# Split rings of four pieces and two more load buffers in both expert stages; two of four output blocks stored plainly

## The chip, the cores and the metric

The kernel runs on one core of one Trainium2 chip. The metric is the device time of one execution in microseconds (us); the median of several executions is compared. A profile of one execution is read beside it: PE is TensorE's matmul queue, PEld its weight loads, DVE VectorE, ACT ScalarE, POOL GpSimd and SP SyncE. In the profile, "SPq" is an instruction by which SP issues a transfer, and L107 is line 107 of the kernel.

## The reference

512 tokens of width 1024 pass through two transformer blocks, all in float32. The first has a mixer of forgetting attention and a gated linear recurrence, and then 16 experts of inner width 512, two for each token. The second has a mixer of neighbourhood attention and grouped-query attention, and then 32 experts of inner width 1024, four for each token. Cut to the two expert parts and the end:

```python
# first block: 16 experts, two of one group of four for each token
for e in range(N_EXPERTS):
    h = jax.nn.silu(t @ w_e_gate[e]) * (t @ w_e_up[e])
    y = y + comb[:, e:e + 1] * (h @ w_e_down[e])
...
# second block: 32 experts, four for each token
def expert_block(args):
    xe, e = args
    gu = xe @ w_gu[e] + b_gu[e]
    x_glu = jnp.minimum(gu[:, :D_FF], SWIGLU_LIMIT)
    x_lin = jnp.clip(gu[:, D_FF:], -SWIGLU_LIMIT, SWIGLU_LIMIT)
    act = (x_lin + 1) * (x_glu * jax.nn.sigmoid(SWIGLU_ALPHA * x_glu))
    return act @ w_dn[e] + b_dn[e]
...
x = x + gt1 * rmsnorm(y, g_post_mix[i])          # after the second mixer
...
x = x + gt2 * rmsnorm(f[:B * S].reshape(B, S, D), g_post_ffn[i])   # the end
```

## The kernel before

**Stages.** By the trace, the first block's mixer runs to about 372 us, its experts from 386 to 724, the second block's mixer to about 1260, its experts from 1269 to 2367, and the end to 2399. The weights of the experts (96 MB in the first stage, 384 in the second) are each read once.

**Loads.** One *step* of an experts' stage is one load of 1 MB by `raw` (L102 to L107) from SP's queue into a buffer `wraw`, and the matmuls with it. `experts` (L1274) writes down the order of all steps in the list `seq`: for each expert the parts "gu" (gate and up) and "dn" (down). `moe_pools` (L960) gives the stage `nraw` buffers, seven in the first stage and nine in the second; RAW is the order in which their places are used. The first loads are issued by SP (AHEAD of them) and by POOL (the rest, in the step that BEHIND names; negative steps lie ahead of the first). From there on load n is issued when step n − `nraw` has given its buffer free (`free`, `load`).

**Splits.** Float32 products are made from split numbers. `split` (L115 to L121) turns half a load, a *half piece* of 128 x 1024, into a high part `whi` (ACT, L120) and the rest `wlo` (DVE, L121). Both have rings of `nsplit` places. A half piece takes three matmuls for each product (`mm3`): high by high, low by high, high by low. The splits are written into the program `ahead` = `nsplit` − 1 half steps ahead of the matmuls that use them (`spl`, `held`; SPL for the first ones). A buffer of a split step is free when both its halves are split. Experts with few tokens (`col`, and `rows` in the second stage: 64 or 32 places) use the load as it is, without a split, and free it when PE has used it.

**Around the matmuls.** `x_gather` (L995) has POOL gather an expert's tokens into `xg`; PE turns them (`x_turn`, L1007), ACT and DVE split them (`x_split`, L1014 to L1018). `act`, `act_turn` and `act_split` (L1136 to L1176) make the activation; `y_scatter` (L1199 to L1212) weighs the result into `eo` on ACT and DVE and POOL adds it into the array `Y` in HBM. `hooks` says in which half step each of these is written into the program; all engines work in program order, each on its own queue. Two experts of each stage (PAIRS) run a second block of 64 places with the same weights.

**The ranking of experts** (L853 and on) runs on POOL, DVE, PE and ACT at the start of each stage, since it decides which expert's weights are loaded where.

**The end.** `tail_norm` (in the second mixer, store at L2147) stores x, 512 tokens in four blocks of 128, into the output. `moe2` (L2190 to L2266) calls `experts` and then reads the sums of the experts (`Y2`) back in four blocks, two from SP and two from ACT (L2250); ACT squares them (L2252); DVE multiplies by the gain (L2256 or L2265) and makes the reciprocal root of two blocks at a time (`rsqrt`, L151 to L161); POOL stores all four blocks with a transfer that adds to the output (L2266). `after` loads the gain row (`RW`, L2238) behind the last weights.

Of the kernel before, what the change touches and what calls it, by code (L numbers as in the profile page):

```python
# [11 lines left out]
F32 = mybir.dt.float32  # L12
F32R = mybir.dt.float32r
# [3 lines left out]
AF = mybir.ActivationFunctionType  # L17
OP = mybir.AluOpType
# [7 lines left out]

FIXED = {2: 2, 1: 2}
PAIRS = {2: (7, 16), 1: (4, 7)}
RAW = {2: (7, 8, 1, 3, 0, 4, 5, 6, 2), 1: (0, 1, 2, 3, 4, 5, 6)}
AHEAD = {2: 6, 1: 4}  # L30
BEHIND = {2: (-11, -11, -11), 1: (-6, -6, -6, -6)}
SPL = {2: (-11, -10.5, -10, -9.5, -9), 1: (-0.5, -0.5, -0.5, -0.5, -0.5)}

PLAN = {2: (0, 1, 2, 3, 4, 5), 1: (-4, -3, -1, 0, 1, 2)}

# [6 lines left out]
class Kern:  # L42
# [129 lines left out]
    def consts(self):  # L172
        nc, cp, t = self.nc, self.cp, self.t
        self.ident = cp.tile([128, 128], F32, name="ident")
        make_identity(nc, self.ident)
        self.identb = cp.tile([128, 128], BF, name="identb")
        nc.vector.tensor_copy(self.identb, self.ident)
        self.onesb = cp.tile([128, 128], BF, name="onesb")
        nc.vector.memset(self.onesb, 1.0)
        self.ones = cp.tile([128, 1], F32, name="ones")  # L180
        nc.vector.memset(self.ones, 1.0)
        jp = cp.tile([128, 128], I32, name="jp")
        nc.gpsimd.iota(jp, pattern=[[1, 128]], base=0, channel_multiplier=-1)
        self.tri = cp.tile([128, 128], BF, name="tri")
        nc.vector.tensor_scalar(self.tri, jp, 0.0, None, op0=OP.is_gt)
        self.mtri = cp.tile([128, 128], BF, name="mtri")
        nc.vector.tensor_scalar(self.mtri, jp, 0.0, -NEG, op0=OP.is_gt, op1=OP.mult)
        self.slots = cp.tile([128, 128], F32, name="slots")
        nc.gpsimd.iota(self.slots, pattern=[[1, 128]], base=0, channel_multiplier=0,
                       allow_small_or_imprecise_dtypes=True)  # L190
        self.pcol = cp.tile([128, 1], F32, name="pcol")
        nc.gpsimd.iota(self.pcol, pattern=[[1, 1]], base=0, channel_multiplier=1,
                       allow_small_or_imprecise_dtypes=True)
        self.trash = cp.tile([128, 1], F32, name="trash")
        nc.vector.tensor_scalar(self.trash, self.pcol, 512.0, None, op0=OP.add)
        rank = cp.tile([32, 48], F32, name="rank")
        nc.gpsimd.dma_start(rank, self.dap(t["rank_c"], 0, [[0, 32], [1, 48]]))
        self.rank = {32: rank[:, 0:32], 16: rank[:, 32:48]}
        self.ntrash = cp.tile([128, 1], F32, name="ntrash")
        nc.vector.tensor_scalar(self.ntrash, self.trash, -1.0, None, op0=OP.mult)  # L200
        self.half = cp.tile([128, 2], F32, name="half")
        nc.vector.memset(self.half, 0.0)
        nc.vector.memset(self.half[64:128, 0:1], 1.0)
        nc.vector.memset(self.half[0:64, 1:2], 1.0)
        self.zero1 = cp.tile([128, 1], F32, name="zero1")
        nc.vector.memset(self.zero1, 0.0)
        self.one1 = cp.tile([128, 1], F32, name="one1")
        nc.vector.memset(self.one1, 1.0)
        self.mod1 = self.dp.tile([6, 1024], F32, name="mod1")
        self.mod2 = self.dp.tile([6, 1024], F32, name="mod2")  # L210
        self.modc = self.dp.tile([2, 1024], F32, name="modc")
        self.X1 = self.dp.tile([512, 1024], F32, name="X1")
        self.U1 = self.dp.tile([512, 1024], F32, name="U1")
        self.U2 = self.dp.tile([512, 1024], F32, name="U2")
        self.Y1 = self.dp.tile([640, 1024], F32, name="Y1")
        self.Y2 = self.dp.tile([640, 1024], F32, name="Y2")
        self.VA = self.dp.tile([512, 512], F32, name="VA")
        self.c1 = self.load_silu([t["c"]])
        self.c2 = self.load_silu([t["c_2"], t["c_ctx_2"]])

# [737 lines left out]


    def moe_pools(self, nh):  # L960
        self.nraw, self.nsplit, self.neo = (7, 9)[nh - 1], 6, nh

        order = RAW[nh]
        low = self.slot_pools(range(self.nraw - 2))
        if nh == 2:
            self.esm = self.pool("e_small", 1)
        self.rings(2048, 0, self.nsplit)
        if nh == 1:
            self.esm = self.pool("e_small", 1)
        self.ex = self.pool("e_x", 2)  # L970
        self.ea = self.pool("e_a", 2)
        high = self.slot_pools(range(self.nraw - 2, self.nraw))
        slots = (low + high)
        it = itertools.cycle([slots[i] for i in order])
        self.rw = type("R", (), {})()
        self.rw.tile = lambda shape, dt, name: next(it).tile(shape, dt, name=name)
# [606 lines left out]
    def mixer2(self):  # L1583
# [555 lines left out]
        def tail_norm(c):  # L2139
# [4 lines left out]
            nc.vector.scalar_tensor_tensor(yc, yc, r, xr[c // 2][:, c % 2, :], op0=OP.mult, op1=OP.add)  # L2144
            nc.gpsimd.tensor_mul(xr[c // 2][:, c % 2, :], yc, rows[1])

            nc.gpsimd.dma_start(self.out[0, cs, :], yc)  # L2147
            q = w4t("q4", 1024)
            nc.scalar.activation(q, yc, AF.Square, accum_out=ss[:, 2 * c + 1:2 * c + 2])
            nc.vector.tensor_copy(rr[:, c:c + 1], self.rsqrt(ss[:, 2 * c + 1:2 * c + 2], 1, 1e-6, 1.0 / 1024))  # L2150
# [40 lines left out]
    def moe2(self):  # L2191
# [39 lines left out]
                self.mm(ps, l.bitcast(F32) if col else l, r.bitcast(F32) if col else r, start, False)  # L2231
            return f
        self.U, self.Y = self.U2, self.Y2
        rows = []

        def after():
            rows.append(self.ea.tile([128, 1024], F32, name="eo", bufs=self.neo))
            nc.sync.dma_start(rows[0], self.dap(self.RW, 2048, [[0, 128], [1, 1024]]))  # L2238

        self.experts(32, src_of, 2, bias_of, (), after)  # L2240

# [1 line left out]
        ss = self.lsm.tile([128, 4], F32, name="ssf")  # L2243
        vs = [self.rw.tile([128, self.wn], F32, name="wraw") for _ in range(4)]
        ys, qs = [v[:, 0:1024] for v in vs], [v[:, 1024:2048] for v in vs]
        d = self.rw.tile([128, self.wn], F32, name="wraw")
        d = [d[:, 0:1024], d[:, 1024:2048], ys[2], ys[3]]
        with self.tc.manual_schedule():
            for c in range(4):
                (nc.scalar if c % 2 else nc.sync).dma_start(ys[c], self.Y2[c * 128:c * 128 + 128, :])  # L2250
            for c in range(4):
                nc.scalar.activation(qs[c], ys[c], AF.Square, accum_out=ss[:, c:c + 1])  # L2252
            for c0 in (0, 2):
                if c0 == 0:
                    for c in (0, 1):
                        nc.vector.tensor_mul(d[c], ys[c], row)  # L2256
                r = self.rsqrt(ss[:, c0:c0 + 2], 2, 1e-6, 1.0 / 1024)
                for c in (c0, c0 + 1):
                    k = r[:, c - c0:c - c0 + 1]
                    if c == 0:  # L2260
                        nc.vector.tensor_scalar(d[c], d[c], k, None, op0=OP.mult)
                    elif c == 1:
                        nc.scalar.activation(d[c], d[c], AF.Copy, scale=k)
                    else:
                        nc.vector.scalar_tensor_tensor(d[c], ys[c], k, row, op0=OP.mult, op1=OP.mult)  # L2265
                    nc.gpsimd.dma_start(self.out[0, c * 128:c * 128 + 128, :], d[c], accum_op=OP.add)  # L2266


_INS = ['x', 'c', 'w_ada', 'b_ada', 'w_in', 'b_f', 'conv_w', 'conv_b', 'w_rg', 'b_rg', 'w_ig', 'b_ig',
# [50 lines left out]
```

## Time and profile before

| | us |
|---|---|
| median of three runs | 2403.52 |
| lowest and highest | 2400.86, 2406.54 |
| the profiled run | 2400.73 |
| its span | 2398.9 |

The profile is one execution. Its times are microseconds from the start of the span; 1.8 us of the run lie around the span. A group of rows says which view it comes from. "idle before <-releaser" in brackets is how long the engine had nothing to do before an instruction, and which instruction or transfer ended that. In the views of DMA, GB/s is what all transfers of the core moved.

### The profile page before, as it was taken

The page shows a single profiled execution, that of the slowest core. Times are in us where ns is not written, and L with a number is a line of the kernel's source. Part 1 is how long each engine was busy: PE and PEld are TensorE (multiplying, and loading weights), DVE is VectorE, ACT ScalarE, POOL GpSimd, SP SyncE. Part 2 cuts the span into 40 slices and gives each one's busy share as a digit, 9 for nine tenths or more (in the row PEclk, how much of TensorE's full clock was granted, in tenths as well). Part 3 has the DMA queues.
Part 4 walks back from the last instruction along what each step waited for, and adds up shares of the span by engine and source line. Part 5 has one row for each costly group of instructions (what it writes and reads, how often), then busy time and mean ns, then how long its engine had stood idle before and what let it go on. Part 6 is the DMA issues. An engine that isn't in the chain of part 4 may idle for free. (4 is left out here: it accounts for less than half of the span.)

```text
span 2398.9 us, 31482 instructions
## 1 busy us (share of the span) xinstructions
PE 2123.2 (89%) x11221; PEld 1360.6 (57%) x11221; DVE 1369.1 (57%) x2676; ACT 1012.0 (42%) x1559; POOL 492.8 (21%) x426
## 2 busy tenths in 40 slices
PE   6999986778897999999978999979999799989983
PEld 2655655445566887778866655635556445536520
DVE  5555697444787856654378655535555365527412
ACT  3332444344673544553236444424444244416301
POOL 2001233311212120000025213311232222114201
PEclk9999997889998999999988999989999999999996
DMA  9767547988986423313448999899999899999997
GB/s 292 234 211 249 182 154 267 348 316 283 321 334 209 98 80 114 103 58 127 145 149 317 346 397 386 355 354 396 398 387 397 308 394 394 395 392 397 389 412 241
DMA packets 208291, 679.29 MB, mean 283 GB/s; under 512 B 21260, under 2 KB 61028, under 8 KB 161024
## 3 DMA queue, kind: packets, MB, share of 16 engines
q1 hardware_dynamic: 185280, 607.88, 67.5%
q0 software_dynamic: 22560, 68.28, 10.5%
q8 instruction: 91, 1.49, 0.3%
q10 hardware_dynamic: 288, 1.05, 0.1%
q14 instruction: 72, 0.59, 0.1%
HBM read 641.51 MB, written 35.72 MB: 282 GB/s over the span
## 5 line engine op out<-in xcount | busy, mean ns | idle before, releaser
L121 DVE TENSOR_TENSOR wlo<-wraw,whi 128x1024 fp32r<-128x1024 f32 (+1 forms) x535 | 642.9, 1234 | 380.0 <-ACT whi L120 372.6
L120 ACT ACTIVATE whi<-wraw 128x1024 fp32r<-128x1024 f32 (+1 forms) x535 | 541.9, 1051 | 375.0 <-DMA wraw<-in_w_gu 129.4
L83 PE MATMUL pm<-whi,xh 128*128 128x512 f32 (+1 forms) x704 | 289.5, 412 | 21.2 <-ACT whi L120 21.2
L83 PE MATMUL pm<-wlo,xh 128*128 128x512 f32 (+1 forms) x704 | 284.5, 407 | 13.7 <-DVE wlo L121 13.5
L83 PE MATMUL pm<-wraw,xh 128*32 128x512 f32 (+1 forms) x1344 | 251.9, 633 | 14.6 <-DMA wraw<-in_w_gu 14.6
L1212 POOL DMA_INDIRECT Y<-eo,isc x52 | 119.2, 2292 | 643.0 <-ACT eo L1211 248.6
L83 PE MATMUL pm<-whi,xl 128*96 128x512 f32 (+1 forms) x608 | 245.7, 404 | 0.0
L83 PEld LDWEIGHTS pm<-whi,xh 128*128 128x128 f32 (+1 forms) x704 | 128.9, 183 | 70.0 <-ACT whi L120 28.9
L995 POOL DMA_INDIRECT xg<-U,ig x52 | 92.4, 1776 | 364.7 <-PE pt L1117 133.0
L83 PEld LDWEIGHTS pm<-wlo,xh 128*128 128x128 f32 (+1 forms) x704 | 122.6, 174 | 60.3 <-DVE wlo L121 23.2
L83 PEld LDWEIGHTS pm<-wraw,xh 128*32 128x32 f32 (+1 forms) x1344 | 65.4, 128 | 140.9 <-issue 106.4
L83 PE MATMUL po<-wraw,ah 128*32 128x512 f32 (+1 forms) x672 | 127.6, 624 | 15.1 <-DMA wraw<-in_w_dn 15.1
L83 PEld LDWEIGHTS pm<-whi,xl 128*96 128x96 f32 (+1 forms) x608 | 109.3, 180 | 34.6 <-issue 0.2
L83 PE MATMUL po<-whi,ah 128*96 128x512 f32 (+1 forms) x304 | 122.2, 402 | 2.6 <-ACT ah L1172 2.5
L83 PE MATMUL po<-whi,al 128*96 128x512 f32 (+1 forms) x304 | 120.1, 395 | 1.8 <-DVE al L1174 1.0
L83 PE MATMUL po<-wlo,ah 128*96 128x512 f32 (+1 forms) x304 | 119.6, 393 | 0.0
L1007 PE MATMUL pt<-ident,xg 64*128 64x64 f32 (+3 forms) x416 | 70.7, 296 | 44.2 <-DMA xg<-U,ig 41.3
L1007 PEld LDWEIGHTS pt<-ident,xg 64*128 64x128 f32 (+3 forms) x416 | 56.9, 199 | 90.6 <-issue 41.1
L1018 DVE TENSOR_TENSOR xl<-pt,xh 128x384 fp32r<-128x384 f32 (+1 forms) x48 | 29.5, 615 | 111.1 <-ACT xh L1016 110.8
L1016 ACT ACTIVATE xh<-pt 128x384 fp32r<-128x384 f32 (+2 forms) x56 | 28.6, 511 | 145.9 <-PE pt L1007 137.1
L83 PEld LDWEIGHTS po<-wraw,ah 128*32 128x32 f32 (+1 forms) x672 | 35.6, 126 | 92.3 <-issue 62.2
L83 PE MATMUL px<-hh,whi 128*128 128x512 f32 x192 | 77.3, 403 | 0.6 <-DVE gsum L765 0.6
(624 smaller groups left out, 3872.4 us busy)
## 6 DMA issues: line engine op xcount, KB each, us to landing
wraw<-in_w_gu SPq DMA_DIRECT2D x254, 1024.0 KB
wraw<-in_w_dn SPq DMA_DIRECT2D x127, 1024.0 KB
wraw<-in_w_e_down SPq DMA_DIRECT2D x32, 1024.0 KB
wraw<-in_w_e_up SPq DMA_DIRECT2D x31, 1024.0 KB
wraw<-in_w_e_gate SPq DMA_DIRECT2D x30, 1024.0 KB
wraw<-in_w_in SPq DMA_DIRECT2D x58, 512.0 KB
mz<-in_w_ada SPq DMA_DIRECT2D x80, 256.0 KB
wraw<-in_w_mod SPq DMA_DIRECT2D x26, 512.0 KB
```

The lines of the kernel that those rows point to most:

```text
L83: self.nc.tensor.matmul(out, lhsT, rhs, start=start, stop=stop)
L120: nc.scalar.activation(h, v, AF.Copy)
L121: nc.vector.tensor_sub(l, v, h.bitcast(F32))
L995: self.nc.gpsimd.indirect_dma_start(out=B.xg[0:B.n, :], out_offset=None, in_=self.U, in_offset=bass.IndirectOffsetOnAxis(ap=B.ig[:, :1], a ...
L1007: self.nc.tensor.transpose(B.xt[:, k * n:k * n + n], B.xg[0:n, 4 * h2 + k:1024:8], self.ident[0:n, 0:n])
L1016: nc.scalar.activation(B.xh[:, d, 0:n], pv, AF.Copy)
L1018: nc.vector.tensor_sub(lo, pv, B.xh[:, d, 0:n].bitcast(F32))
L1212: nc.gpsimd.indirect_dma_start(out=self.Y[:, :], out_offset=bass.IndirectOffsetOnAxis(ap=B.isc[:, :1], axis=0), in_=o, in_offset=None, com ...
```

## The change

- `nraw` is 9 and 11 in place of 7 and 9, `nsplit` is 4 in place of 6. In each partition a buffer takes 8 KB and so does one place of both rings together, so the space is the same. RAW names the new order of the buffers.
- POOL issues five loads at the start of each stage in place of three (BEHIND); three half pieces are split ahead of the first matmul in place of five (SPL).
- A new array X3 in HBM takes blocks 0 and 2 of x from `tail_norm`; blocks 1 and 3 go to the output as before. `after` loads X3 by SP behind the gain row.
- At the end DVE multiplies all four blocks by the gain first, then makes one reciprocal root of four columns. Blocks 0 and 2: DVE multiplies by the root, adds x and SP stores plainly. Blocks 1 and 3: ACT multiplies by the root and POOL stores with the adding transfer.

```diff
--- before.py
+++ after.py
@@ -26,10 +26,10 @@
 
 FIXED = {2: 2, 1: 2}
 PAIRS = {2: (7, 16), 1: (4, 7)}
-RAW = {2: (7, 8, 1, 3, 0, 4, 5, 6, 2), 1: (0, 1, 2, 3, 4, 5, 6)}
+RAW = {2: (9, 10, 1, 3, 0, 4, 5, 6, 2, 7, 8), 1: (0, 1, 2, 3, 4, 5, 6, 7, 8)}
 AHEAD = {2: 6, 1: 4}
-BEHIND = {2: (-11, -11, -11), 1: (-6, -6, -6, -6)}
-SPL = {2: (-11, -10.5, -10, -9.5, -9), 1: (-0.5, -0.5, -0.5, -0.5, -0.5)}
+BEHIND = {2: (-11, -11, -11, -11, -11), 1: (-6, -6, -6, -6, -6)}
+SPL = {2: (-11, -10.5, -10), 1: (-0.5, -0.5, -0.5)}
 
 PLAN = {2: (0, 1, 2, 3, 4, 5), 1: (-4, -3, -1, 0, 1, 2)}
 
@@ -215,6 +215,7 @@
         self.Y1 = self.dp.tile([640, 1024], F32, name="Y1")
         self.Y2 = self.dp.tile([640, 1024], F32, name="Y2")
         self.VA = self.dp.tile([512, 512], F32, name="VA")
+        self.X3 = self.dp.tile([256, 1024], F32, name="X3")
         self.c1 = self.load_silu([t["c"]])
         self.c2 = self.load_silu([t["c_2"], t["c_ctx_2"]])
 
@@ -958,7 +959,7 @@
 
 
     def moe_pools(self, nh):
-        self.nraw, self.nsplit, self.neo = (7, 9)[nh - 1], 6, nh
+        self.nraw, self.nsplit, self.neo = (9, 11)[nh - 1], 4, nh
 
         order = RAW[nh]
         low = self.slot_pools(range(self.nraw - 2))
@@ -2144,7 +2145,7 @@
             nc.vector.scalar_tensor_tensor(yc, yc, r, xr[c // 2][:, c % 2, :], op0=OP.mult, op1=OP.add)
             nc.gpsimd.tensor_mul(xr[c // 2][:, c % 2, :], yc, rows[1])
 
-            nc.gpsimd.dma_start(self.out[0, cs, :], yc)
+            nc.gpsimd.dma_start(self.out[0, cs, :] if c % 2 else self.X3[c * 64:c * 64 + 128, :], yc)
             q = w4t("q4", 1024)
             nc.scalar.activation(q, yc, AF.Square, accum_out=ss[:, 2 * c + 1:2 * c + 2])
             nc.vector.tensor_copy(rr[:, c:c + 1], self.rsqrt(ss[:, 2 * c + 1:2 * c + 2], 1, 1e-6, 1.0 / 1024))
@@ -2231,11 +2232,15 @@
                 self.mm(ps, l.bitcast(F32) if col else l, r.bitcast(F32) if col else r, start, False)
             return f
         self.U, self.Y = self.U2, self.Y2
-        rows = []
+        rows, xs = [], []
 
         def after():
             rows.append(self.ea.tile([128, 1024], F32, name="eo", bufs=self.neo))
             nc.sync.dma_start(rows[0], self.dap(self.RW, 2048, [[0, 128], [1, 1024]]))
+            xs.append(self.ex.tile([128, 1024], F32, name="xg"))
+            xs.append(self.ex.tile([128, 8, 128], F32R, name="xh", bufs=3).bitcast(F32).rearrange("p k q -> p (k q)"))
+            for i in range(2):
+                nc.sync.dma_start(xs[i], self.X3[i * 128:i * 128 + 128, :])
 
         self.experts(32, src_of, 2, bias_of, (), after)
 
@@ -2243,27 +2248,25 @@
         ss = self.lsm.tile([128, 4], F32, name="ssf")
         vs = [self.rw.tile([128, self.wn], F32, name="wraw") for _ in range(4)]
         ys, qs = [v[:, 0:1024] for v in vs], [v[:, 1024:2048] for v in vs]
-        d = self.rw.tile([128, self.wn], F32, name="wraw")
-        d = [d[:, 0:1024], d[:, 1024:2048], ys[2], ys[3]]
+        d = [self.rw.tile([128, self.wn], F32, name="wraw") for _ in range(2)]
+        d = [v[:, 1024 * a:1024 * a + 1024] for v in d for a in range(2)]
         with self.tc.manual_schedule():
             for c in range(4):
                 (nc.scalar if c % 2 else nc.sync).dma_start(ys[c], self.Y2[c * 128:c * 128 + 128, :])
             for c in range(4):
                 nc.scalar.activation(qs[c], ys[c], AF.Square, accum_out=ss[:, c:c + 1])
-            for c0 in (0, 2):
-                if c0 == 0:
-                    for c in (0, 1):
-                        nc.vector.tensor_mul(d[c], ys[c], row)
-                r = self.rsqrt(ss[:, c0:c0 + 2], 2, 1e-6, 1.0 / 1024)
-                for c in (c0, c0 + 1):
-                    k = r[:, c - c0:c - c0 + 1]
-                    if c == 0:
-                        nc.vector.tensor_scalar(d[c], d[c], k, None, op0=OP.mult)
-                    elif c == 1:
-                        nc.scalar.activation(d[c], d[c], AF.Copy, scale=k)
-                    else:
-                        nc.vector.scalar_tensor_tensor(d[c], ys[c], k, row, op0=OP.mult, op1=OP.mult)
-                    nc.gpsimd.dma_start(self.out[0, c * 128:c * 128 + 128, :], d[c], accum_op=OP.add)
+            for c in range(4):
+                nc.vector.tensor_mul(d[c], ys[c], row)
+            r = self.rsqrt(ss, 4, 1e-6, 1.0 / 1024)
+            for c in range(4):
+                k = r[:, c:c + 1]
+                o = self.out[0, c * 128:c * 128 + 128, :]
+                if c % 2:
+                    nc.scalar.activation(d[c], d[c], AF.Copy, scale=k)
+                    nc.gpsimd.dma_start(o, d[c], accum_op=OP.add)
+                else:
+                    nc.vector.scalar_tensor_tensor(ys[c], d[c], k, xs[c // 2], op0=OP.mult, op1=OP.add)
+                    nc.sync.dma_start(o, ys[c])
 
 
 _INS = ['x', 'c', 'w_ada', 'b_ada', 'w_in', 'b_f', 'conv_w', 'conv_b', 'w_rg', 'b_rg', 'w_ig', 'b_ig',
```

## Rows read from the trace of the kernel before

**Rows 1.** The page: busy share of the DMA engines, 40 slices of 60 us

```profile
DMA  9767547988986423313448999899999899999997
```

**Rows 2.** Busy PE, PEld, DVE, ACT, POOL, then PEclk, DMA share, GB/s by window

```profile
1380.00:2360.00 980.00, 886.88 (x4287) 484.54 (x4289) 487.14 (x693) 381.68 (x488) 223.32 (x147) 0.96 1.00 385
386.00:724.00 338.00, 289.80 (x1404) 190.64 (x1402) 209.64 (x348) 181.31 (x258) 77.81 (x62) 0.91 0.89 321
```

**Rows 3.** The same view: inside the two pair experts of the second stage

```profile
1551.00:1561.00 10.00, 10.00 (x58) 6.21 (x56) 4.89 (x2) 1.69 (x2) 6.63 (x5) 1.00 0.10 35
1869.00:1879.00 10.00, 10.00 (x58) 6.10 (x57) 4.84 (x2) 0.86 (x1) 5.82 (x5) 1.00 0.11 28
```

**Rows 4.** Timeline of SP's queue at the first pair; GB/s, 40 slices of 1540:1580

```profile
1545.62 0.33 SPq L107 DMA_DIRECT2D wraw<-in_w_gu  x1
1560.62 0.33 SPq L107 DMA_DIRECT2D wraw<-in_w_gu  x1
GB/s 340 422 418 434 418 434 418 434 434 418 352 188 127 21 0 0 0 0 0 0 16 98 270 418 336 254 385 369 418 418 410 426 442 426 418 418 451 336 164 303
```

**Rows 5.** Windows view again: the start of the second experts' stage

```profile
1280.00:1360.00 80.00, 77.37 (x406) 58.91 (x405) 59.48 (x70) 50.33 (x62) 32.52 (x22) 1.00 0.92 327
```

**Rows 6.** Timeline of POOL ahead of both stages: start, us, engine, line, operation

```profile
377.63 0.58 POOL L107 DMA_DIRECT2D wraw<-in_w_e_gate  x1
1269.39 1.07 POOL L995 DMA_INDIRECT xg<-U,ig  x1 [3.34 <-PE pt L1007]
```

**Rows 7.** Timeline of PE, four waits of the first stage; brackets: idle before, releaser

```profile
469.03 0.68 PE L1158 MATMUL pt<-ident,eb 32*128 32x32 f32 x4 [6.29 <-ACT pt L1544]
494.07 0.74 PE L1158 MATMUL pt<-ident,ea 64*128 64x64 f32 x4 [6.04 <-ACT xh L1014]
570.44 0.74 PE L1158 MATMUL pt<-ident,ea 64*128 64x64 f32 x4 [6.11 <-DVE al L1176]
618.05 0.41 PE L83 MATMUL pt<-paux,oh 128*96 128x6 bf16 x4 [3.55 <-ACT xh L1014]
```

**Rows 8.** Timeline of ACT ahead of the end of the second of these waits

```profile
491.13 1.99 ACT L120 ACTIVATE whi<-wraw 128x1024 fp32r<-128x1024 f32 x2
493.14 0.60 ACT L1172 ACTIVATE ah<-pt 128x512 fp32r<-128x512 f32 x1
493.64 0.38 ACT L1014 ACTIVATE xh<-pt 128x256 f32<-128x256 f32 x1
```

**Rows 9.** Groups of splits, 640 to 712 us, and PE's timeline, one matmul triple

```profile
L121 DVE TENSOR_TENSOR wlo<-wraw,whi 128x1024 fp32r<-128x1024 f32 x44 | 52.0, 1219 | 9.1 <-ACT whi L120 9.0
L120 ACT ACTIVATE whi<-wraw 128x1024 fp32r<-128x1024 f32 x44 | 44.8, 1056 | 14.6 <-DMA wraw<-in_w_e_gate 7.2 <-DMA wraw<-in_w_e_up 3.7 <-PE po L83 1.1
611.81 0.39 PE L83 MATMUL pm<-wlo,xh 128*96 128x512 f32 x1
612.50 0.39 PE L83 MATMUL pm<-wlo,xh 128*96 128x512 f32 x1
```

**Rows 10.** DMA issues: gathers of both stages, count, KB or us to landing

```profile
xg<-U,ig POOLq DMA_INDIRECT x16, 6.7
xg<-U,ig POOLq DMA_INDIRECT x29, 9.8
```

**Rows 11.** Timeline of the end; GB/s, 40 slices of 2374:2382 and of 2385:2398

```profile
2377.66 2.36 DVE L2256 TENSOR_TENSOR wraw<-wraw,eo 128x1024 f32<-128x1024 f32 x2 [7.98 <-DMA wraw<-Y]
2381.82 1.06 ACT L2252 ACTIVATE wraw<-wraw 128x1024 f32<-128x1024 f32 x1 [1.89 <-DMA wraw<-Y]
2384.04 0.18 DVE L151 TENSOR_SCALAR rs<-ssf 128x2 f32<-128x2 f32 x1 [1.08 <-ACT wraw L2252]
2386.30 2.48 DVE L2265 SCALAR_TENSOR_TENSOR wraw<-wraw,rs,eo 128x1024 f32<-128x1024 f32 x2
GB/s 0 0 0 0 0 41 225 184 61 328 492 410 348 328 430 369 451 451 369 389 492 369 369 471 451 348 328 492 328 328 532 410 328 328 41 41 20 20 0 0
GB/s 0 151 126 126 202 214 227 214 202 227 176 202 202 189 214 227 202 189 214 202 202 176 202 202 176 214 202 176 189 189 214 227 139 38 0 0 0 0 0 0
```

**Rows 12.** Timeline of SP's queue behind the first pair

```profile
1587.89 11.15 SPq L107 DMA_DIRECT2D wraw<-in_w_gu  x1
```

## The prediction

> **What bounds the kernel now.** I read the page's line of DMA shares first: it is at its top in slices 9 to 12 and nearly all the way from slice 22 on [rows 1]; these are the two experts' stages. The windows view says what this means in each. In the second stage (1269 to 2367 us) the 16 DMA engines are busy 1.00 of the time at 385 GB/s, while PE has 887 of 980 us of work [rows 2]. So DMA sets the pace there, and only a time at which DMA has nothing to do can be won back. In the first stage (386 to 724 us) DMA stands at 0.89 and PE at 290 of 338 us [rows 2]: neither is full, and each short stall has to be looked at by itself.
>
> Where is DMA idle in the second stage? The windows view with 10 us windows shows two holes, one in each expert that runs a second block (the pairs): PE works 10.00 of 10 us and DMA 0.10 and 0.11 [rows 3]. SP's timeline gives the reason: one load is issued at 1545.62, the next at 1560.62 [rows 4]. A load waits for the buffer that the load nine places earlier used; up to 1560 all nine buffers are loaded or in use, the queue runs dry near 1551, and PE is busy with the pair. A third, smaller loss lies at the start: DMA is at 0.92 in the 80 us from 1280 [rows 5].
>
> **The change, part by part.**
>
> *Two more buffers, second stage, pairs.* Load n now waits for step n−11, not n−9. The pair's splits still free buffers while PE works, but the buffers ahead of it run out two loads later. Around the first pair the GB/s line of the DMA view shows 418 to 434 GB/s while loads flow [rows 4], so a load of 1.05 MB takes 2.5 us, and two fill 5.0 us of the 10 us hole. The stage is bound by DMA on both sides of the hole, so every load behind it, and the end, comes 5.0 us earlier. Two pairs: **−10.0**. Lower bound of the gain: splits run two half pieces (one load) later with the short ring, and where the buffers come from splits the net is one load in place of two, so −2.5 each, −5.0 in all. Upper bound: 2.7 us a load at the stage's mean of 385 GB/s [rows 2], −10.9.
>
> *The same at the start of the second stage.* 0.08 of 80 us is 6.4 us of idle DMA [rows 5]. Two loads more ahead are worth 5.0, but they can't win more than the idle there is, and PE works 77.4 of these 80 us, so part of it could come back as PE's own time. I take **−5.0**, ends 0 and −6.4. The first matmuls wait for a gather, and POOL issues the two added loads ahead of it, at 0.58 us each by the first stage's row; POOL's idle of 3.34 us before that gather covers 1.2 us of it [rows 6]. If the cover were gone it would cost +1.2.
>
> *The first stage, its start.* POOL issues five loads in place of three before it starts the ranking that the plan of the experts needs; one issue takes 0.58 us and the ranking follows at once [rows 6]. PE's first expert waits for that chain: **+1.2**.
>
> *The first stage, shorter ring.* The split of a piece (ACT for the high part, DVE for the rest) is written in program order 5 half pieces ahead of its use; now it is 3. ACT and DVE work in order, so what stands behind a burst of splits waits for it. PE has four waits of 3.55 to 6.29 us that end on such an operation: three on ACT, one on DVE [rows 7]. It is the turned input or activation of a small expert, in the first one a norm for the next mixer. In the second wait two high parts, 1.99 us together, run on ACT right ahead of the operations PE needs [rows 8]; the other three have the same picture. With lead 3 two of the splits move behind them: about 2.0 us if ACT is late, 2.4 if DVE is (two of 1219 ns [rows 9]), and I take 2.2 for each of four: **−8.8**. Ends: nothing, if another wait ends at the same time, and −9.6.
>
> *The first stage, fuller queues.* With two loads more in flight, DMA's 0.89 rises a little, and gathers share it: from issue to landing a gather takes 6.7 us here and 9.8 us in the second stage with DMA at 1.00 [rows 10]. A shift of the share by 0.02 of the 0.11 between them is 0.6 us a transfer, and PE's or ACT's long waits end on three gathers or scatters here: **+1.7**. Ends: 0, and +9.3 (3.1 each). This stage too has holes in DMA (0.11 of 338 us [rows 2]), but PE doesn't wait for loads behind them: filling them is worth nothing in my sum, with −5.0 (a pair's gain in the other stage) as the other end.
>
> *Does the ring of four starve PE?* At the tightest place (640 to 712 us) a high part takes 1056 ns and a low part 1219 [rows 9]: 2.3 us from buffer to ready. PE needs 0.69 us for three matmuls [rows 9], and a half piece has six, 1.38 us. Three pieces ahead are 4.1 us, more than 2.3. So no stall in a steady run, with 1.8 us to spare, where five pieces gave 4.6. I set it at nothing, with an upper end of +4 for this stage; in the second one DMA is the bound.
>
> *The end.* Before, all four results are accumulated into the output from POOL's queue. In the DMA view that runs at about 200 GB/s, while the plain loads of the Y rows come at about 400 [rows 11]: 2.6 us and 1.3 us for 0.52 MB. The accumulates begin in the second slice of 0.325 us behind 2385 and end in the 34th, at 2396.05 [rows 11]. Now, step by step: the first two products are made in 2.36 us from 2377.66; the third and fourth wait for rows that arrive at 2381.82, and end at 2384.2. One reciprocal root over four columns takes as long as the one that starts at 2384.04 and ends at 2386.30, 2.3 us, to 2386.5. The first multiply-and-add is 1.24 us (half of 2.48) [rows 11], so the first store is issued at 2387.7 and flows about 2 us later, as before: 2389.7. Two plain and two accumulated blocks take 2 × 1.3 + 2 × 2.6 = 7.8 us, to 2397.5 against 2396.05: +1.4 if they add up. If plain packets run in the gaps of the accumulating ones, four times 1.3 would do, 2394.9, or −1.2. The Y rows, issued from two queues, moved about 400 GB/s, no more than SP's queue alone at the pair [rows 4, 11]; a plain and an accumulating transfer side by side are in no row. The Trainium skill ("DMA: Bandwidth & Descriptors", section "Issuing engines are not separate DMA queues") says that transfers started on several engines run on the same 16 DMA engines and only save issue time; by that rule the end would cost the whole +1.4. I take **+0.8**, nearer to adding up, ends −1.5 and +1.5. The two loads of X3 (1 MB, 2.5 us) stand behind the last weights and land before the Y rows are issued: nothing. The stores to X3 replace stores of the same size: nothing.
>
> **Sum:** −10.0 −5.0 +1.2 −8.8 +1.7 +0.8 = −20.1 us. The profiled run took 2400.73 us, its span 2398.9 and 1.8 around it; the median of the three is 2403.52, 2.8 above the profiled one. A difference holds for either, so I subtract from the median: 2383.4.
>
> **The rivals.**
>
> *Second stage only.* The first stage's waits come from another cause that comes as late (a scatter, the other engine), so the −8.8 are not there; the rest is −11.3: 2392.2. For it: ACT and DVE both have splits in front, so one may come as late as the other. Against: where the row shows it, the splits are the very last thing in front [rows 8], and both engines lose two of them.
>
> *Loads can't be put in flight.* Two more buffers help only if SP can issue into them. Behind the first pair one issue took 11.15 us where its neighbours take 0.33 [rows 4, 12]: with many loads outstanding, SP blocks. If the queue held no more than it does now, a free buffer would be worth nothing at the pairs' rims; but when the hole begins the queue is empty, so only that part of the gain goes that is not yet issued when DMA runs dry. With one load of two, the three places give −2.5 each and the rest stands: −12.6, 2390.9. The Trainium skill ("Perfetto Trace Analysis", section "DMA Instruction — HWDGE (DVE, Sync)") says that an engine starts early when more descriptors are made than its buffer holds; it gives no depth, and the long issue fits a full buffer.
>
> *Slower: the short ring starves PE.* Wherever ACT or DVE is held up in the first stage (by a gather, a scatter, the step from a small expert to a split one), five pieces of cover were 6.9 us, three are 4.1: a hold longer than that reaches PE 2.8 us earlier. Without the −8.8 the rest of the sum is −11.3, so 4 such holds use it up (4 × 2.8 = 11.2). With one in every second of the 16 experts it is 8 × 2.8 − 11.3 = +11.1: 2414.6. For it: DVE is the longest helper and works in order. Against: 1.8 us to spare in the tightest run, and DMA, not PE, is the bound in most of the second stage.
>
> **How the numbers follow.** Forecast (both stages gain) 0.5: 2383.4, with its own range of 2374 to 2391. Second stage only 0.2: 2392. Loads not in flight 0.14: 2391. Starved ring 0.09: 2414.6; the rest (parts cancel) 0.07: 2401. To leave out no more than 2 in 10 I take 2373 to 2400. Less than 0.2% (4.8 us) is about what can't be told from no change here. Faster than 2398.7: 0.81; within: 0.1; slower than 2408.3: 0.09.
>
> **What would show it.** In the pairs DMA must be idle for 5 us where it was 10, and the gap on SP must shrink to about 10 us. In the first stage PE's four waits must be 2 us shorter. At the end two stores must be seen on SP's queue and the last bytes at 2397.5 less the gain ahead. Wrong would be: PE waiting for a high or low part where it did not, or an SP queue that is blocked when DMA runs dry.

## The result and the profile after

| | before | after |
|---|---|---|
| median, us | 2402.19 | 2377.99 |
| lowest and highest of four | 2399.26, 2406.54 | 2377.08, 2381.31 |
| profiled run: span | 2398.9 | 2379.5 |

The kernel before has a fourth run here, so its median is 1.3 us below the one that the forecast started from. The ratio of the times is 0.990 (95% interval 0.9881 to 0.9919): 24 us less, where 20 were forecast. The profiled run of the changed kernel is the longest of its four; its span is only 19.4 us shorter. Read by stages, from the timeline of PE (the start of its first matmul with a weight of a stage to the start of its last), that is put right:

| us | before | after | difference |
|---|---|---|---|
| up to the first gather of the first experts' stage | 374.2 | 379.6 | +5.4 |
| from there to PE's first such matmul | 11.75 | 11.91 | +0.2 |
| first experts' stage | 336.9 | 323.2 | −13.7 |
| second mixer, to PE's first matmul of the next stage | 546.6 | 547.1 | +0.5 |
| second experts' stage | 1096.5 | 1082.4 | −14.1 |
| to the loads of Y | 8.3 | 8.3 | 0.0 |
| from the loads of Y to the end of the span | 24.7 | 26.9 | +2.3 |

The first line has nothing to do with the change: that part holds the same work, and over the profiles of all the kernels below it took 374.2 to 379.6 us. So the two experts' stages carry the gain, 14 us each.

The page of the changed kernel, its line of DMA shares in 40 slices:

```profile
DMA  8767446988976423323448999999999999999996
```

From slice 23 on DMA is full as before [rows 1], and the slices of the two pairs (26 and 32), which were at 8, are at 9. The windows view of the changed kernel (the columns of rows 2): the first stage, the start of the second, and 16 us about the hole of each pair:

```profile
391.00:715.00 324.00, 288.55 (x1406) 190.21 (x1405) 210.69 (x348) 183.27 (x258) 74.38 (x62) 0.93 0.92 335
1272.00:1352.00 80.00, 76.61 (x388) 58.07 (x387) 60.65 (x71) 50.31 (x60) 27.97 (x20) 1.00 0.97 350
1539.00:1555.00 16.00, 15.29 (x88) 8.63 (x87) 6.66 (x5) 4.51 (x8) 7.77 (x7) 1.00 0.57 210
1849.00:1865.00 16.00, 15.32 (x87) 9.10 (x89) 6.16 (x5) 4.51 (x8) 7.75 (x7) 1.00 0.79 297
```

And the two holes in the kernel before, with windows placed by the same step of the stage (rows 3 have only their cores):

```profile
1549.00:1565.00 16.00, 16.00 (x93) 9.46 (x92) 7.05 (x6) 5.45 (x8) 8.29 (x7) 1.00 0.40 140
1866.00:1882.00 16.00, 16.00 (x93) 9.46 (x92) 7.05 (x5) 5.36 (x8) 8.47 (x7) 1.00 0.38 137
```

DMA's idle time in such a window is 16 us times what is missing from 1.00. The first hole goes from 9.6 to 6.9 us, the second from 9.9 to 3.4, in all 9.2 us less; the 80 us at the start go from 0.92 [rows 5] to 0.97, 4.0 us less. Together that is 13.2 of the 14.1 us by which the stage is shorter. On SP's timeline at the first pair, where 15.0 us lay between two loads [rows 4], it is now 11.7. The run with short rings and nine buffers, below, tells what of this is the rings' and what the buffers':

```profile
1535.09 0.33 SPq L107 DMA_DIRECT2D wraw<-in_w_gu  x1
...
1546.80 0.33 SPq L107 DMA_DIRECT2D wraw<-in_w_gu  x1
```

In the first stage the view of PE's waits (us in total, times, longest) tells the story, before:

```profile
PE pm L83 <- ACT whi L120: 9.8, 3, 7.1
PE pt L1007 <- DMA xg<-U,ig: 6.7, 1, 6.7
PE pt L1158 <- ACT pt L1544: 6.3, 1, 6.3
PE pt L1158 <- DVE al L1176: 6.1, 1, 6.1
PE pt L1158 <- ACT xh L1014: 6.0, 1, 6.0
PE pt L83 <- ACT xh L1014: 4.4, 2, 3.6
```

and after:

```profile
PE pm L83 <- ACT whi L120: 10.2, 2, 7.3
PE pt L1008 <- DMA xg<-U,ig: 7.2, 1, 7.2
PE pt L1159 <- DVE ea L1153: 5.0, 2, 4.7
PE pt L1159 <- DVE al L1177: 3.8, 1, 3.8
PE pt L1159 <- ACT pt L1545: 2.2, 1, 2.2
PE pt L83 <- ACT xh L1015: 0.4, 1, 0.4
```

The waits on the turned inputs and activations (ACT pt, DVE al, ACT xh, DVE ea) are less; those on a high part and on a gather are still there, a little longer. PE's four waits of rows 7 in the timeline of the changed kernel (the last is gone):

```profile
471.66 0.66 PE L1159 MATMUL pt<-ident,eb 32*128 32x32 f32 x4 [2.19 <-ACT pt L1545]
...
497.31 0.72 PE L1159 MATMUL pt<-ident,ea 64*128 64x64 f32 x4 [4.72 <-DVE ea L1153]
...
567.53 0.69 PE L1159 MATMUL pt<-ident,ea 64*128 64x64 f32 x4 [3.84 <-DVE al L1177]
...
612.36 0.30 PE L83 MATMUL pt<-paux,oh 128*96 128x6 bf16 x4
```

6.29, 6.04, 6.11 and 3.55 us have become 2.19, 4.72, 3.84 and none: 11.2 us less. ACT's timeline at the second of them shows the two high parts, which stood ahead of these operations [rows 8], now behind them:

```profile
495.81 0.60 ACT L1173 ACTIVATE ah<-pt 128x512 fp32r<-128x512 f32 x1
496.30 0.38 ACT L1015 ACTIVATE xh<-pt 128x256 f32<-128x256 f32 x1
496.57 2.00 ACT L120 ACTIVATE whi<-wraw 128x1024 fp32r<-128x1024 f32 x2
```

The end, in the timeline of the changed kernel, and GB/s in 40 slices of 2364 to 2379.5:

```profile
2352.52 0.80 SPq L2255 DMA_DIRECT2D wraw<-Y  x2
...
2357.92 2.36 DVE L2259 TENSOR_TENSOR wraw<-wraw,eo 128x1024 f32<-128x1024 f32 x2 [9.98 <-DMA wraw<-Y]
...
2366.95 1.53 SPq L2269 DMA_DIRECT2D out<-wraw  x2
2367.08 1.90 POOL L2266 DMA_DIRECT2D out<-wraw  x2 [17.53 <-DVE wraw L2268]
...
GB/s 0 0 0 0 0 0 0 0 0 137 370 423 381 212 0 233 233 275 264 254 254 275 222 254 233 222 148 233 211 190 233 159 0 0 0 0 0 0 0 0
```

The two plain stores are on SP's queue, the two adding ones on POOL's. The data move at up to 423 GB/s while only the first plain block flows, and at 150 to 275 behind it, where the adding transfers and the second plain block flow together.

### The profile page after: what moved, and what is told of

It reads as the page before. It is cut to its first block, busy times and chain, and to the rows that moved or that the text cites. A ratio compares the mean times of both kernels' runs of the same rounds, so it can differ in the third digit from the quotient of the medians.

```text
span 2379.5 us, 31516 instructions
## 1 busy us (share of the span) xinstructions
PE 2120.2 (89%) x11221; PEld 1356.1 (57%) x11221; DVE 1371.5 (58%) x2665; ACT 1017.6 (43%) x1560; POOL 509.2 (21%) x428
## 5 line engine op out<-in xcount | busy, mean ns | idle before, releaser
L83 PE MATMUL pm<-whi,xh 128*128 128x512 f32 (+1 forms) x704 | 286.6, 408 | 14.9 <-ACT whi L120 14.4
L83 PE MATMUL pm<-wraw,xh 128*32 128x512 f32 (+1 forms) x1344 | 254.4, 637 | 21.5 <-DMA wraw<-in_w_gu 21.5
L1213 POOL DMA_INDIRECT Y<-eo,isc x52 | 109.7, 2110 | 603.3 <-ACT eo L1212 240.2
L996 POOL DMA_INDIRECT xg<-U,ig x52 | 127.7, 2456 | 316.9 <-issue 154.2
```

Of the source, the lines that this page charges most:

```text
L83: self.nc.tensor.matmul(out, lhsT, rhs, start=start, stop=stop)
L996: self.nc.gpsimd.indirect_dma_start(out=B.xg[0:B.n, :], out_offset=None, in_=self.U, in_offset=bass.IndirectOffsetOnAxis(ap=B.ig[:, :1], a ...
L1213: nc.gpsimd.indirect_dma_start(out=self.Y[:, :], out_offset=bass.IndirectOffsetOnAxis(ap=B.isc[:, :1], axis=0), in_=o, in_offset=None, com ...
```

## The experiments

The times of a kernel are compared with runs of the kernel before on the same chip (2404.88, 2404.26 and 2405.85 us in the three sessions). The ratio is given with its 95% interval; it is not the quotient of the two medians and can differ from it by 0.2%. Of each edit the main lines stand here; RAW, BEHIND and SPL follow the numbers of buffers and places. The edits of the last two kernels are against the changed kernel, the others against the kernel before. Stage lengths are read as in the table above. In profiles of kernels that leave it as before, the first stage took 332.9 to 338.1 us and the second 1096.1 to 1096.8. The end is judged by the runs, because from the loads of Y on, the old end alone took 24.7 to 27.3 us in the profiles.

**Each part alone.** Three kernels take over one part of the change each, a fourth both stages without the end. The second stage alone:

```diff
-        self.nraw, self.nsplit, self.neo = (7, 9)[nh - 1], 6, nh
+        self.nraw, self.nsplit, self.neo = (7, 11)[nh - 1], (6, 4)[nh - 1], nh
```

> Only the second expert stage has 11 load buffers and split rings of four; the first stage and the end are as before. My theory: the two added loads fill part of the holes in DMA in the pairs and at the stage's start, as the trace of the changed kernel has it: 14 us less than before (the stage from its first matmul to its last 14 us shorter, the first stage within 1 us of before). Rival, the extra loads are held back by a full queue or by later splits: 7 us less at most, and DMA idle for 7 us or more in each pair.

2390.14 us, ratio 0.9932 (0.9915 to 0.995): 14.7 us less by the medians, 12 to 20 by the interval. The second stage took 1080.1 us, 16.4 less (1079.3 to 1082.4 in all five profiles that have it so); the first 337.6, as before. The holes of the pairs hold 0.57 and 0.78 of DMA work in their 16 us, as in the changed kernel. The rival of a blocked queue (7 us at most) falls.

The first stage alone:

```diff
+        self.nraw, self.nsplit, self.neo = (9, 9)[nh - 1], (4, 6)[nh - 1], nh
```

> Only the first expert stage has nine load buffers and split rings of four. My theory: shorter bursts of splits ahead of what PE waits for, so the first stage is 13.6 us shorter, as in the trace of the changed kernel, and the run 13 us faster; the second stage unchanged. Rival, part of those 13.6 us was a lucky run of that one profile: the 5.9 us of my forecast or less.

2389.9 us, ratio 0.9939 (0.9919 to 0.9959). The first stage took 322.8 us, 14.1 less, the second 1096.8. So the 13.7 us were no accident of one profile, and the rival of a gain in the second stage only falls too.

The end alone (X3, its loads, the new order of the last products), with both stages' rings as before:

```diff
-            nc.gpsimd.dma_start(self.out[0, cs, :], yc)
+            nc.gpsimd.dma_start(self.out[0, cs, :] if c % 2 else self.X3[c * 64:c * 64 + 128, :], yc)
...
+                if c % 2:
+                    nc.scalar.activation(d[c], d[c], AF.Copy, scale=k)
+                    nc.gpsimd.dma_start(o, d[c], accum_op=OP.add)
+                else:
+                    nc.vector.scalar_tensor_tensor(ys[c], d[c], k, xs[c // 2], op0=OP.mult, op1=OP.add)
+                    nc.sync.dma_start(o, ys[c])
```

> Only the end is changed (two blocks stored plainly with x read back from X3); both expert stages as before. If plain and adding transfers add up on the DMA engines, the end is slower by 1.3 to 2.4 us from the loads of Y to the end of the span, and the run slower by the same. Rival, the 2.3 us that the end lost in the changed kernel's profile came from late Y rows in that run: 0 to 0.5 us.

2405.28 us, ratio 1.0003 (0.9993 to 1.0014), that is +0.7 us with ends of −1.7 and +3.4. The end from the loads of Y took 25.7 us here, inside what the old end takes. The 2.3 us of the first comparison came from two profiles at the two sides of that scatter: Y's first rows landed 3.4 us after their issue in the one and 5.4 in the other. DVE starts as they land (2377.66 before [rows 11], 2357.92 after); the issue before:

```profile
2374.24 0.81 SPq L2250 DMA_DIRECT2D wraw<-Y  x2
```

Counted from that start, the new end took 21.5 us in the changed kernel and 21.9 here, the old one 21.2 to 22.6 in nine profiles. What the new end costs can't be told from nothing.

Both stages, old end:

```diff
-        self.nraw, self.nsplit, self.neo = (7, 9)[nh - 1], 6, nh
+        self.nraw, self.nsplit, self.neo = (9, 11)[nh - 1], (4, 4)[nh - 1], nh
```

> Both expert stages as in the changed kernel, the end as before. If the parts add up and the end costs 2.3 us, this is 26 to 27 us faster than before, 2.3 us faster than the changed kernel. Rival, the end costs nothing: 24 us faster than before, the same as the changed kernel.

2376.27 us, ratio 0.9879 (0.9862 to 0.9895): 28.6 us less, with an interval of 25 to 33. The two stages took 322.5 and 1082.4 us. The parts add up (14.7 and 15.0). The changed kernel's interval (0.9881 to 0.9919) overlaps with this one, so this pair doesn't settle the end either.

**What it is in the first stage: order, ring or loads?** A ring of four and the shorter lead, with seven loads as before:

```diff
-        self.nraw, self.nsplit, self.neo = (7, 9)[nh - 1], 6, nh
+        self.nraw, self.nsplit, self.neo = (7, 9)[nh - 1], (4, 6)[nh - 1], nh
```

> Only the first stage's rings of split weights are short (four places, three half pieces ahead); it keeps its seven load buffers. My theory: the first stage gains by the order of the splits alone, so it is 9 to 14 us shorter than before's 336.9 us. Rival, the gain comes from the two added load buffers and the short ring starves PE: the stage is as long as before or up to 10 us longer, with new waits of PE for high or low parts.

2392.73 us, ratio 0.9934 (0.9909 to 0.9959); the stage took 323.8 us, 13.2 less. The added load buffers are worth next to nothing in this stage (322.8 with them).

The shorter lead with rings of six:

```diff
-        ahead, nraw = self.nsplit - 1, self.nraw
+        ahead, nraw = (3, 5)[nh - 1], self.nraw
```

> Only the place of the splits in the program is changed, in the first stage: three half pieces ahead of their use in place of five, with rings of six places and seven load buffers as before. If the order on ACT and DVE is what matters, this stage is 9 to 14 us shorter, the same as with the ring of four within 1 us. Rival, the ring's size matters (a split starts when a place is free): no gain here, or more than 2 us away from the run with the ring of four.

2387.99 us, ratio 0.9928 (0.9905 to 0.9951). The stage took 320.5 us, 16.4 less, with these waits of PE:

```profile
PE pm L83 <- ACT whi L120: 8.5, 2, 7.5
PE pt L1158 <- DVE ea L1152: 5.2, 2, 4.7
PE pt L1158 <- DVE al L1176: 3.8, 1, 3.8
PE pt L1158 <- ACT pt L1544: 2.2, 1, 2.2
```

These are the waits of the changed kernel, with the ring's size as before: where the splits are written in the program is what counts most. The stage is 3.3 us shorter than with the ring of four, past the 2 us that I had set as the rival's mark, so the ring's size is not ruled out as a second, smaller cause. Part of the 3.3 us is PE's speed, which differs from profile to profile; the sum of PE's idle time in the stage is steadier (gaps over 0.25 us added up from the timeline). It is 45.4 to 47.1 us in the five profiles that leave the stage as before, 33.9 us here, 34.8 in the last kernel below, which has the same first stage, and 34.7 to 36.9 in the five profiles with the ring of four. So the order takes 8 to 13 us from PE's waits, whichever ring; what the ring's size adds to them is 3 us at most. The stage itself took 320.5 and 317.2 us with rings of six and 322.5 to 323.8 with rings of four; whether that is the ring's size or PE's speed, these runs leave open.

The lead of two:

```diff
+        ahead, nraw = (2, 5)[nh - 1], self.nraw
```

> Only the place of the splits in the first stage is changed: two half pieces ahead of their use, rings of six, seven load buffers. If order is all that counts in this stage, it gains the 16 us of the lead of three again or up to 5 us more, as one split less stands ahead of what PE waits for. Rival, the lead becomes too short: a high and a low part take 2.3 us and two half pieces of PE 2.8, so each hold of ACT or DVE reaches PE, and the stage is longer than the 320.5 us of the lead of three by 3 us or more.

2387.58 us, ratio 0.992 (0.9903 to 0.9938); the stage took 323.2 us with 35.0 us of idle PE, between what the theories said. The longest wait on ACT's high part was 8.2 us, where the lead of three had 7.5. In sum the waits on high parts grew from 8.5 to 12.2 us, while the one on ACT pt is gone. Two pieces are as good as three in the runs.

**What it is in the second stage.** Short rings with nine loads:

```diff
+        self.nraw, self.nsplit, self.neo = (7, 9)[nh - 1], (6, 4)[nh - 1], nh
```

> Only the second stage's rings are short; it keeps its nine load buffers. My theory: splits run one load later, so buffers come free later, and each hole in DMA (pairs, start) grows by up to 2.5 us: the stage 0 to 8 us longer than before's 1096.5. Rival, the order of the splits is worth something here as in the first stage: 3 us shorter or more.

2408.15 us, ratio 1.0016 (1.0001 to 1.0031), that is 0.2 to 7.5 us more, while in the profile the stage took 1094.5 us, 2.0 less; in the same profile the two mixers took 2.4 and 3.3 us more. The windows of this run at the start and at the holes:

```profile
1286.00:1366.00 80.00, 76.56 (x386) 58.21 (x388) 60.87 (x71) 50.34 (x61) 27.97 (x20) 1.00 0.91 317
1556.00:1572.00 16.00, 15.30 (x89) 8.71 (x87) 6.64 (x5) 4.49 (x7) 7.77 (x7) 1.00 0.45 163
1870.00:1886.00 16.00, 15.32 (x84) 9.29 (x84) 6.29 (x5) 4.54 (x8) 7.75 (x7) 1.00 0.48 173
```

0.91, 0.45 and 0.48, where the kernel before has 0.92 [rows 5], 0.40 and 0.38: the holes are 8.8 and 8.3 us, 0.8 and 1.6 less than before. The shorter rings alone save no time that the runs show. But SP's timeline at the first pair has the shorter interval already:

```profile
1552.18 0.33 SPq L107 DMA_DIRECT2D wraw<-in_w_gu  x1
...
1563.89 0.33 SPq L107 DMA_DIRECT2D wraw<-in_w_gu  x1
```

It is 11.7 us with nine buffers and short rings, as in the changed kernel, and 15.0 with nine buffers and long rings. So the interval came with the rings, in which the splits stand later in the program, and not with the buffers; that later splits would free buffers later, as I had it, doesn't show. What the two buffers add is the step from this run to the run with this stage alone changed: 1094.5 to 1080.1 us. In the changed kernel the holes are 6.9 and 3.4 us in place of the 8.8 and 8.3 here. Most of this stage's gain is the buffers' own.

One buffer more and rings of five, half of the step:

```diff
+        self.nraw, self.nsplit, self.neo = (7, 10)[nh - 1], (6, 5)[nh - 1], nh
```

> Only the second stage is changed, with ten load buffers and rings of five (four half pieces ahead): half of the step. If every buffer is worth one load of 2.5 us at each of three places, the stage gains half of the 14 to 17 us: 7 to 8 us less than 1096.5. Rival, what counts is a threshold (the second buffer alone brings the gain, or the first): under 4 us or over 12.

2389.91 us, ratio 0.9939 (0.9918 to 0.9961), and its profile also has a first stage that is 4 us short (332.9 us, unchanged work). The second stage took 1085.3 us, 11.2 less: more than half, less than all.

```profile
1277.00:1357.00 80.00, 77.38 (x407) 59.20 (x406) 60.62 (x71) 51.14 (x62) 33.37 (x22) 1.00 0.97 345
1542.00:1558.00 16.00, 16.00 (x93) 9.47 (x92) 6.91 (x6) 5.50 (x10) 7.77 (x7) 1.00 0.62 235
1855.00:1871.00 16.00, 16.00 (x92) 9.48 (x91) 6.89 (x6) 5.50 (x10) 7.75 (x7) 1.00 0.63 245
```

The start has its whole gain with one buffer (0.97, 4.0 us); the holes have 6.1 and 5.9 us of idle DMA, 3.5 and 4.0 less than before. Again the sum, 11.5, is the gain. So the other half of the step, an eleventh buffer and rings of four, works on the second pair only (5.9 to 3.4 us; the first one has 6.9). Why the first hole doesn't go on shrinking is not settled by these runs.

**The end, without adding transfers.** All four blocks stored plainly by SP, all of x kept in X3, two of the products made on POOL, roots by twos; stages as changed:

```diff
-            for c in range(4):
-                nc.vector.tensor_mul(d[c], ys[c], row)
-            r = self.rsqrt(ss, 4, 1e-6, 1.0 / 1024)
+            for c in (2, 3):
+                nc.gpsimd.tensor_mul(d[c], ys[c], row)
+            for c in (0, 1):
+                nc.vector.tensor_mul(d[c], ys[c], row)
+            for c0 in (0, 2):
+                r = self.rsqrt(ss[:, c0:c0 + 2], 2, 1e-6, 1.0 / 1024)
...
+                    nc.vector.scalar_tensor_tensor(ys[c], d[c], r[:, c - c0:c - c0 + 1], xs[c], op0=OP.mult, op1=OP.add)
+                    nc.sync.dma_start(self.out[0, c * 128:c * 128 + 128, :], ys[c])
```

> Both expert stages as in the changed kernel; at the end all four blocks are stored plainly by SP, all of x is read back from HBM, two of the products with the gain are made on POOL, and the roots are made by twos as before. If the adding transfers (2.6 us for 0.52 MB against 1.3) set the end, from the loads of Y to the end of the span it takes 3 to 4 us less than the 24.7 to 27.1 of the other ends, and the run is 27 us faster than before or more. Rival, the end is bound by the work on DVE and ACT: no more than 1 us less.

2373.81 us, ratio 0.9861 (0.9841 to 0.9882), but from the loads of Y to the end it took 25.2 us, not 3 us less than the others. The timeline of DVE and POOL says why:

```profile
2355.99 0.16 DVE L158 TENSOR_TENSOR rs<-rs,rs 128x2 f32<-128x2 f32 x1
2356.02 4.66 POOL L2260 TENSOR_TENSOR wraw<-wraw,eo 128x1024 f32<-128x1024 f32 x2 [11.92 <-DVE rs L157]
2356.19 2.21 DVE L161 SCALAR_TENSOR_TENSOR rs<-rs,rs 128x2 f32<-128x2 f32 x1
2358.43 2.26 DVE L157 TENSOR_TENSOR rs<-rs 128x2 f32<-128x2 f32 x1
```

While POOL makes its two products (4.66 us), two of DVE's tiny steps of the root take 2.21 and 2.26 us in place of 0.16: 4.2 us more on the way to the stores that wait for this root.

**A version that beats both.** First stage with lead three, rings of six and seven loads; second stage as changed; all four blocks stored plainly, with every product on DVE and one root:

```diff
-        self.nraw, self.nsplit, self.neo = (9, 11)[nh - 1], 4, nh
+        self.nraw, self.nsplit, self.neo = (7, 11)[nh - 1], (6, 4)[nh - 1], nh
...
-        ahead, nraw = self.nsplit - 1, self.nraw
+        ahead, nraw = (3, 3)[nh - 1], self.nraw
...
-                if c % 2:
-                    nc.scalar.activation(d[c], d[c], AF.Copy, scale=k)
-                    nc.gpsimd.dma_start(o, d[c], accum_op=OP.add)
-                else:
-                    nc.vector.scalar_tensor_tensor(ys[c], d[c], k, xs[c // 2], op0=OP.mult, op1=OP.add)
-                    nc.sync.dma_start(o, ys[c])
+                nc.vector.scalar_tensor_tensor(ys[c], d[c], k, xs[c], op0=OP.mult, op1=OP.add)
+                nc.sync.dma_start(o, ys[c])
```

> A version meant to beat both: first stage with seven load buffers and rings of six, but splits three half pieces ahead; second stage as in the changed kernel; the end with one root of four columns and all products on DVE, all four blocks stored plainly by SP. My theory, adding up the stages of the earlier runs: first stage 16 us less than before, second 14 to 17 less, end 3 us less (22 to 23 us from the loads of Y to the end of the span): 33 to 36 us less than before. Rival, the parts don't add up or the end is bound elsewhere: 30 us less or under.

2369.63 us, ratio 0.985 (0.9834 to 0.9867): 36 us less than before, and its interval lies below the changed kernel's. The stages took 317.2 and 1081.9 us, the end 22.3 (GB/s in 40 slices of 2352 to 2362.2):

```profile
2339.94 1.09 SPq L2256 DMA_DIRECT2D wraw<-Y  x2
...
2354.65 3.92 SPq L2266 DMA_DIRECT2D out<-wraw  x4
2355.73 2.48 DVE L2265 SCALAR_TENSOR_TENSOR wraw<-wraw,rs,xh 128x1024 f32<-128x1024 f32 x2
...
GB/s 0 0 0 0 0 0 0 0 0 0 0 0 0 193 418 386 402 386 402 402 434 434 353 418 386 434 353 450 418 386 402 386 450 337 0 0 0 0 0 0
```

The stores now flow at 350 to 450 GB/s without a break. Two profiles with all stores plain (25.2 with the blocked root, 22.3 without) against eleven with adding transfers in them (24.7 to 27.3): here the end is shorter than any of them. Counted from the landing of Y's first rows it took 18.1 us here and 21.2 to 22.6 in the twelve others. The two plain ends differ in the number of roots too, so no run has the blocked root alone.

## Why the prediction was right, step by step

- **Pairs, −10.0.** Right in place, and in size partly by luck: 9.2 us of DMA's holes are filled (2.7 and 6.5), and the stage shortens by what DMA no longer idles. But 2.4 of the 9.2 us came with the short rings, from which the prediction expected a loss or nothing; the buffers filled 6.8. That both pairs give 5.0 was too even. The interval between two loads on SP, which I had named as a sign of the buffers' work, is a sign of the shorter rings.
- **Start of the second stage, −5.0.** Mechanism right; 4.0 by DMA's share. A single buffer gives the same.
- **Start of the first stage, +1.2.** Wrong: +0.2. I read the issue times on POOL and took what follows for the critical chain, but POOL had a wait of its own a little later that took them up. Before and after, POOL's timeline:

```profile
381.28 0.33 POOL L861 TENSOR_SCALAR planm<-rank,planc 16x16 f32<-16x16 f32 x1 [1.21 <-DVE planc L860]
```

```profile
384.09 0.58 POOL L107 DMA_DIRECT2D wraw<-in_w_e_down  x1
...
386.85 0.33 POOL L862 TENSOR_SCALAR planm<-rank,planc 16x16 f32<-16x16 f32 x1 [0.34 <-DVE planc L861]
```

The wait on DVE's planc was 1.21 us and is 0.34 now. It stood in the trace of before, a few rows further on; a chain has to be followed to the first wait on another engine before an added step is priced.
- **Shorter lead in the first stage, −8.8.** The mechanism was right, and the two runs that separate it (the ring of four alone, the lead alone) confirm it; the term was too small. The four waits lost 11.2 us, but unevenly: 4.1, 1.3, 2.3 and 3.6 in their order, where 2.2 was taken for each. The third is the picture of the prediction: two low parts of 2.35 us together stood ahead of `al` on DVE and now stand behind it. In the second the two high parts moved likewise, but the wait now ends on another operation of DVE (`ea`). In the first and the fourth the picture doesn't hold: right ahead of what PE needs, ACT has one and three high parts before and two and three after. At the fourth, the splits held ACT up through DVE: two low parts stood ahead of the weighing of a result there, for which ACT waits before its next operation. ACT before and after:

```profile
613.69 0.68 ACT L1203 ACTIVATE eo<-po,slw 32x512 f32<-32x512 f32 x1 [2.42 <-DVE eo L1204]
```

```profile
607.99 0.68 ACT L1204 ACTIVATE eo<-po,slw 32x512 f32<-32x512 f32 x1 [0.81 <-DVE eo L1205]
```

That is 1.6 of its 3.6 us; what else the first and the fourth lost is not shown. The stage lost 13.7; PE's idle time is 11.9 of it (47.1 to 35.2). The rest is PE's busy time: the granted clock over the stage is 0.91 before [rows 2] and 0.93 after.
- **Fuller queues, +1.7.** Small, as forecast: the gather's wait grew from 6.7 to 7.2 us, those on a high part from 9.8 to 10.2 in sum. That the fuller queues did this is not shown: in other profiles with seven loads they are 6.7 to 6.9 and 8.5 to 12.2.
- **Ring of four at no cost.** Right. The rival that it starves PE would have shown new waits for high and low parts: 11.8 us before (9.8 and 2.0 on ACT and DVE), 12.6 after.
- **End, +0.8.** Within what the runs allow (+0.7, −1.7 to +3.4), and no more can be said. The blocks did add up on the DMA engines: the part with adding transfers ran at the low rate, with the second plain store inside it.
- **The rivals.** Second stage only: no, the first gains as much by itself. Loads that can't be put in flight: no; with the rings alike, two more buffers took 14.4 us from the second stage, where this rival allowed 7.5. SP's issues take long at many places of the stage, before (up to 12.97 us) and after (up to 10.31), and during the one of 11.15 us [rows 12] DMA was full (1.03 from 1587 to 1600 us). Starved ring: no.

The time, 2378.0, lies 5.4 us below the forecast of 2383.4. Of these, 1.3 us are the median of before, which moved; the rest is the first stage: forecast −5.9 (+1.2 −8.8 +1.7), measured −13.5, of which the other stages and the end gave some back.

## What to carry to other kernels

How far ahead of its use a preparation step is written is a choice of order on in-order engines, apart from how many buffers it has: measure the lead alone before paying for rings. The room that the shorter rings gave back was worth most as load buffers in the stage bound by DMA, and the gain came out as the idle time of DMA that went (13.2 of 14.1 us). Change one of the two at a time: a sign in the trace, as the interval between two loads here, can belong to the other one.

## What the runs showed of the hardware

- A product on POOL stopped DVE: steps of 0.16 us took 2.2 us beside POOL's two multiplications of 128 x 1024, which took 4.66 us together. The Trainium skill ("SBUF — State Buffer", section "Who interferes with whom") says that a DVE instruction with two inputs from SBUF contends with a POOL instruction that reads SBUF; the trace agrees (2.21 and 2.26 us in place of 0.16), even for operands of two columns.
- Adding transfers ran at about 200 GB/s [rows 11] where plain ones of the same shape ran at about 400. It is the adding and not POOL's queue: two plain stores of 512 KB each from that queue, in the second mixer of the changed kernel (L2148 and L2164, 1226 to 1229 us), moved together at 355 to 437 GB/s in most slices.
- The same first mixer took 374.2 to 379.6 us in different runs, and the first stage without any change 332.9 to 338.1; the second stage, bound by DMA, repeated to 0.7 us as it was before and to 3.1 us as changed. Differences in the time of a stage bound by PE need more than one profile.
